# Feed-forward of a decoder trunk: units 4 and 5 with one level of Winograd's scheme in place of two, and three bundles of VectorE work dealt out over the products

## The chip, the cores and the metric

One core of a Trainium2 chip runs the whole program. Its engines work side by side, each through its own list of instructions in the order in which they were written: TensorE (PE, with its weight loads shown as PEld), VectorE (DVE), ScalarE (ACT), GpSimd (POOL) and SyncE (SP). The metric is the device time of one execution in microseconds, lower is better.

## The reference, cut to what matters

```python
for i in range(DEPTH):                                   # 2 layers
    h = rms_norm(x, mix_norm[i])
    x = x + (short_conv_mixer(h, ...), dilated_attention_mixer(h, ...))[i % 2]
    h = rms_norm(x, ffn_norm[i])
    x = x + (silu(h @ w_gate[i]) * (h @ w_up[i])) @ w_down[i]
return rms_norm(x, final_norm)
```

There are 1024 tokens of width 1024, in float32. `w_gate` and `w_up` are 1024 x 2816, `w_down` is 2816 x 1024. The change touches the product of `h` with `w_gate` and `w_up` in the two feed-forwards; the convolution and the attention between them keep their code.

## The kernel before, in words

Every float32 operand is split in a high and a low part (`split`, L128 to L140: ScalarE copies the high part at L138, VectorE subtracts it from the operand at L139, which leaves the low part), and each product of two operands is made of three matmuls: high by high, high by low, low by high (L533, L534, L535).

**Units.** 22 units cover the 2816 columns of the two matrices: unit `u` is 256 columns, of `w_gate` for an even `u` and of `w_up` for the odd `u` after it, multiplied with all tokens. A unit is not computed directly but by Winograd's form of Strassen's scheme: the weights and the tokens are cut in two by two blocks, and seven products of sums of blocks, numbered 1 to 7, replace eight products of blocks. One such product, written (unit, number) here, is 128 columns of weights by 512 rows by 512 tokens: four blocks of rows by three matmuls, so 12 matmuls of 512 columns each. `summed` (L193) makes the sums of weight blocks (L186, `combo`), `part` (L204) splits them (into a tile `w`). The sums of token blocks, the seven operands `self.b[m]`, are made once per feed-forward.

**Two levels.** `whole` (L575) computes a unit with one level, all seven products. The units 0 to 3 of each feed-forward are of this kind. From unit 4 on, two units go together: `shallow` (L597) makes the products 1, 6, 5, 7 and 3 of each, and the products 2 and 4 of both units are made by a second level of the same scheme (`deeper`, L614; its products stand in the order as 11 to 17). A second-level product is 12 matmuls of 256 columns (L625, L627, L628). Its weight operands are sums of quarter blocks (L230), all eight of which are issued when product 5 of the odd unit is prepared (`early`, L243), and its token operands are made out of `self.b[2]` and `self.b[4]` by `deepen` (L637): sums at L641, which the source calls `deep`, then splits into tiles `t` and back into a part of `b`, one step of this generator after each product.

**Evacuation.** After a product ScalarE saves a bank of PSUM where a later product goes on adding to it (`save`, L537 and L539, tile `part`), VectorE adds banks to saved tiles (`add`, L542 and L543; L611 in `shallow`), ScalarE applies Silu to the gate's results (L1137) and VectorE multiplies gate and up (L1140). When all four blocks of a pair of units are there, `store` (L688) makes four sums of them (L704) for the next matrix product and sends them to DRAM from GpSimd's queue (L715). `run(self.store(...))` at L1141 issues these four sums in one go.

**What sets the order.** Nothing is scheduled by a machine. `unit_order` (L252) lists the products; `products` (L561) walks the list. Before product `n` is issued, `take` (L167) has the weights of the products up to `n + 2` prepared (in `deeper` up to three more), so a product's `w` stands on ScalarE's and VectorE's lists two to three products ahead of its matmuls, behind whatever else was issued until then. After product `n`, `filled` (L784) lets each generator in `prep` take one step: `deepen(2)` is put there ten products ahead of (3, 4) (L789), `deepen(4)` one ahead of it (L791).

Counted from 0 in each feed-forward, the products that matter here are: 17 is (1, 3), 18 to 20 are (2, 6), (2, 5), (2, 7), then (3, 6), (2, 4), (2, 3), (3, 5), (3, 7), (4, 1), (3, 4), (3, 3), and 29 to 36 are (4, 6), (4, 5), (4, 7), (5, 1), (4, 3), (5, 6), (5, 5), (5, 7). Product 37, (5, 11), is the first of the second level; the last product of the units is (21, 14), number 180.

## Time and profile before

| what | value |
|---|---|
| median of 3 runs | 2198.8 us (2198.76 to 2199.12) |
| profiled execution, its own time | 2194.63 us |
| its span, first to last instruction | 2192.6 us |
| busy: PE, DVE, ACT, POOL | 2133.3, 1759.4, 999.8, 161.9 us |
| mean granted TensorE clock | 0.992 of full speed |
| first feed-forward, first product to first down product | about 352.6 to 778 us |
| second feed-forward, the same | about 1538 to 1959 us |

A row of the timeline gives the start from the span's beginning, the length, engine, line, operation, tiles written and read, shapes, the number of merged instructions, and in brackets how long the engine sat idle before it and which instruction ended that. Matmuls are pipelined: the length shown is longer than the distance from one start to the next, so their price is read from starts. A row of the windows gives a stretch, its length, the busy time of each engine in it with the number of instructions, the granted TensorE clock, and the load on the DMA engines. The waits list says who waited for whom: total, times, longest.

### The profile page before, as it was taken

The page shows a single profiled execution, that of the slowest core. Times are in us where ns is not written, and L with a number is a line of the kernel's source. Part 1 is how long each engine was busy: PE and PEld are TensorE (multiplying, and loading weights), DVE is VectorE, ACT ScalarE, POOL GpSimd, SP SyncE. Part 2 cuts the span into 40 slices and gives each one's busy share as a digit, 9 for nine tenths or more (in the row PEclk, how much of TensorE's full clock was granted, in tenths as well). Part 3 has the DMA queues.
Part 4 walks back from the last instruction along what each step waited for, and adds up shares of the span by engine and source line. Part 5 has one row for each costly group of instructions (what it writes and reads, how often), then busy time and mean ns, then how long its engine had stood idle before and what let it go on. Part 6 is the DMA issues. An engine that isn't in the chain of part 4 may idle for free.

```text
span 2192.6 us, 30554 instructions
## 1 busy us (share of the span) xinstructions
PE 2133.3 (97%) x11138; PEld 1821.9 (83%) x11138; DVE 1759.4 (80%) x3239; ACT 999.8 (46%) x1812; POOL 161.9 (7%) x212
## 2 busy tenths in 40 slices
PE   7899999999999999999999999999999999999998
PEld 6788888778888878878999999887778888888887
DVE  7797848988888798965677777769988888889886
ACT  6433426444443444434455555525544444454435
POOL 0000001010101000010111111110000101000000
PEclk9999999999999999999999999999999999999999
DMA  4122543222323374423333333544223333365432
GB/s 155 54 83 75 204 156 92 97 92 97 120 97 120 93 280 144 132 82 132 91 91 91 91 91 84 170 124 165 71 77 106 108 103 107 100 234 194 159 91 78
DMA packets 133568, 259.50 MB, mean 118 GB/s; under 512 B 47642, under 2 KB 58922, under 8 KB 133418
## 3 DMA queue, kind: packets, MB, share of 16 engines
q1 hardware_dynamic: 75978, 184.80, 26.1%
q0 software_dynamic: 16272, 49.65, 6.4%
q10 hardware_dynamic: 41168, 23.10, 3.5%
q8 instruction: 88, 1.44, 0.3%
q14 instruction: 62, 0.51, 0.1%
HBM read 187.04 MB, written 66.26 MB: 116 GB/s over the span
## 4 chain that ended last, share of the span: by engine, by line
PE 78%; DVE 13%; ACT 4%; DMA 3%; issue 2%; ACTq 0%; SPq 0%; DVEq 0%
PE bank L533 15%; PE bank L535 15%; PE bank L534 15%; PE bank L349 5%; PE bank L347 5%; PE bank L348 5%; PE bank L1463 4%; PE bank L625 3%; PE bank L627 3%; PE bank L628 3%; DVE w L139 2%; DVE b L526 1%; DVE combo L186 1%; PE bank L1391 1%; PE bank L1390 1%
## 5 line engine op out<-in xcount | busy, mean ns | idle before, releaser
L533 PE MATMUL bank<-b,w 128*128 128x512 f32 x1784 | 704.6, 395 | 25.7 <-DVE part L543 6.4
L535 PE MATMUL bank<-b,w 128*128 128x512 f32 x1784 | 700.7, 393 | 8.7 <-DVE w L139 8.7
L534 PE MATMUL bank<-b,w 128*128 128x512 f32 x1784 | 701.2, 393 | 0.0
L533 PEld LDWEIGHTS bank<-b,w 128*128 128x128 f32 x1784 | 338.8, 190 | 102.1 <-ACT part L539 7.5
L535 PEld LDWEIGHTS bank<-b,w 128*128 128x128 f32 x1784 | 338.7, 190 | 84.1 <-DVE w L139 12.7
L534 PEld LDWEIGHTS bank<-b,w 128*128 128x128 f32 x1784 | 338.5, 190 | 69.7 <-issue 0.7
L138 ACT ACTIVATE w<-combo 128x512 fp32r<-128x512 f32 (+2 forms) x464 | 234.5, 534 | 281.2 <-DVE combo L186 275.2
L139 DVE TENSOR_TENSOR w<-combo,w 128x512 fp32r<-128x512 f32 (+2 forms) x464 | 260.2, 574 | 57.6 <-ACT w L138 56.0
L539 ACT ACTIVATE part<-bank 128x512 f32<-128x512 f32 x168 | 99.5, 593 | 270.2 <-PE bank L535 265.1
L139 DVE TENSOR_TENSOR w<-raw,w 128x512 fp32r<-128x512 f32 (+2 forms) x316 | 169.1, 559 | 17.2 <-ACT w L138 15.6
L543 DVE TENSOR_TENSOR part<-part,bank 128x256 f32<-128x256 f32 (+1 forms) x348 | 158.5, 485 | 26.5 <-PE bank L535 14.3
L138 ACT ACTIVATE w<-raw 128x512 fp32r<-128x512 f32 (+2 forms) x316 | 150.6, 519 | 46.4 <-PE bank L535 11.2
L754 DVE TENSOR_TENSOR x<-x,bank 128x512 f32<-128x512 f32 x168 | 114.2, 680 | 31.1 <-PE bank L535 31.0
L347 PE MATMUL bank<-w_hi,w 128*128 128x512 f32 (+1 forms) x320 | 119.8, 374 | 2.6 <-ACT w L138 2.6
L349 PE MATMUL bank<-w_hi,w 128*128 128x512 f32 (+1 forms) x320 | 118.1, 369 | 0.7 <-DVE w L139 0.7
L348 PE MATMUL bank<-w_lo,w 128*128 128x512 f32 (+1 forms) x320 | 117.8, 368 | 0.0
L466 DVE TENSOR_TENSOR x<-x,bank 128x512 f32<-128x512 f32 (+1 forms) x104 | 66.0, 641 | 60.5 <-PE bank L349 52.2
L186 DVE TENSOR_TENSOR combo<-raw 128x512 f32<-128x512 f32 (+1 forms) x160 | 102.9, 643 | 3.8 <-DMA raw<-in_conv_w_in 3.8
L347 PE MATMUL bank<-h_hi,w_hi 128*128 128x512 f32 x256 | 104.6, 409 | 0.0
L349 PE MATMUL bank<-h_hi,w_lo 128*128 128x512 f32 x256 | 100.2, 391 | 0.7 <-DVE w_lo L139 0.7
L348 PE MATMUL bank<-h_lo,w_hi 128*128 128x512 f32 x256 | 99.9, 390 | 0.0
L1137 ACT ACTIVATE part<-part 128x512 f32<-128x512 f32 x66 | 39.7, 628 | 109.7 <-DVE part L543 109.7
(249 smaller groups left out, 3835.2 us busy)
## 6 DMA issues: line engine op xcount, KB each, us to landing
hin<-part SPq DMA_DIRECT2D x126, 256.0 KB
raw<-in_ffn_w_gate SPq DMA_DIRECT2D x44, 512.0 KB
raw<-in_ffn_w_up SPq DMA_DIRECT2D x44, 512.0 KB
part<-sum POOLq DMA_DIRECT2D x72, 256.0 KB, 2.7
raw<-in_ffn_w_down SPq DMA_DIRECT2D x48, 384.0 KB
x<-spill SPq DMA_DIRECT2D x24, 512.0 KB
raw<-in_attn_w_qkv SPq DMA_DIRECT2D x24, 512.0 KB
raw<-in_conv_w_in SPq DMA_DIRECT2D x21, 512.0 KB
```

Of the source, the lines that this page charges most:

```text
L138: nc.scalar.activation(hi, src, AF.Copy)
L139: eng.tensor_tensor(out=lo, in0=src, in1=hi, op=ALU.subtract)
L186: eng.tensor_tensor(out=c, in0=a, in1=b, op=op)
L347: nc.tensor.matmul(b, whi[:, a], ahi[:, s], start=first, stop=False)
L348: nc.tensor.matmul(b, whi[:, a], alo[:, s], start=False, stop=False)
L349: nc.tensor.matmul(b, wlo[:, a], ahi[:, s], start=False, stop=last)
L533: nc.tensor.matmul(b, hi[:, a], bhi, start=start and k == 0, stop=False, skip_group_check=True)
L534: nc.tensor.matmul(b, hi[:, a], blo, start=False, stop=False, skip_group_check=True)
L535: nc.tensor.matmul(b, lo[:, a], bhi, start=False, stop=k == n - 1, skip_group_check=True)
L539: nc.scalar.activation(t, b, AF.Copy)
L543: nc.vector.tensor_tensor(out=t, in0=t, in1=b, op=ALU.add)
L754: nc.vector.tensor_tensor(out=X[n][:, half(h)], in0=X[n][:, half(h)], in1=b, op=ALU.add)
```

## The change

Five edits, all in the feed-forward's products:

1. `SIMPLE = 6` takes the place of the constants 3 and 4 that bounded the one-level units. Units 4 and 5 become one-level units: products 2 and 4 of each are made whole, and the 14 entries of their second level fall away. Second-level pairs are now (6, 7) to (20, 21), eight per feed-forward where there were nine. The list of products has 178 entries where it had 181.
2. `deepen(2)` is put in after (2, 7) and `deepen(4)` after (4, 5), that is after products 20 and 30 where it was 17 and 26. The last step of each, which overwrites a part of `b`, waits until the last one-level product that reads that operand, (5, 2) or (5, 4), has been issued.
3. The sums of quarter blocks (now L231) are no longer made in one go: one fourth when product 5 of the odd unit is prepared, and one fourth after each of the second level's weights 1, 2 and 5.
4. `store` yields once before its first sum. What is left of it goes into a queue `self.sums`, of which `filled` takes one step after each product, so the four sums (now L712) and their transfers come over the five products that follow.
5. The distances at which weights are loaded from DRAM for units 4 and 5 follow the one-level rule.

```diff
+SIMPLE = 6
...
+        steps = zip(*[sums_of(j, m) for j, m in enumerate(DEEP)])
+
         def part(i):
             load_raw(upto(i))
             w = page("w", F32R)
-            return [split(source(m, i), (w[:, j * HALF:j * HALF + 256], w[:, j * HALF + 256:j * HALF + HALF]),
-                          nc.vector)
-                    for j, m in enumerate(DEEP)]
+            w = [split(source(m, i), (w[:, j * HALF:j * HALF + 256], w[:, j * HALF + 256:j * HALF + HALF]),
+                       nc.vector)
+                 for j, m in enumerate(DEEP)]
+            if i in DEEP_ORDER[:3]:
+                next(steps)
+            return w
 
         def early(op):
             w = op()
-            run(*[sums_of(j, m) for j, m in enumerate(DEEP)])
+            next(steps)
             return w
...
-            for u in range(4, nu, 2):
+            for u in range(4, SIMPLE):
+                order += [(u, 6), (u, 5), (u, 7), (u + 1, 1), (u, 2), (u, 4), (u, 3)]
+            for u in range(SIMPLE, nu, 2):
                 order += [(u, 6), (u, 5), (u, 7), (u + 1, 1), (u, 3), (u + 1, 6), (u + 1, 5), (u + 1, 7)]
...
-            if u < 4 or key == CONV:
+            if u < SIMPLE or key == CONV:
                 a = ((2, 5), (3, 7), (4, 7), (4, 9))[u] if u < 4 else (2 * u + 3, 2 * u + 3)
...
-                ahead = {m: 2 * u + a for m, a in {1: 0 if u > 4 else 3, 6: 1, 5: 2, 7: 3, 3: 3}.items()}
+                ahead = {m: 2 * u + a for m, a in {1: 0, 6: 1, 5: 2, 7: 3, 3: 3}.items()}
...
-            if key != CONV and u > 4 and u % 2:
+            if key != CONV and u > SIMPLE and u % 2:
                 add_deep(units[u], key, u, [[base + r - 2 * (1 - v) for r in rows] for v in range(2)],
...
-                elif self.key != CONV and u > 3:
+                elif self.key != CONV and u >= SIMPLE:
                     self.shallow(u, m, d)
...
-            while self.now <= self.order.index((3, m)):
+            while self.now <= self.order.index((SIMPLE - 1, m)):
                 yield
...
+            yield
             make(7, b22, b12, ALU.subtract)
             yield
...
                     self.now = n + 1
-                    i = self.order.index((3, 4))
-                    if n == i - 10:
+                    if self.order[n] == (2, 7):
                         prep.append(self.deepen(2))
-                    if n == i - 1:
+                    if self.order[n] == (4, 5):
                         prep.append(self.deepen(4))
                     for p in prep:
                         next(p, None)
+                    if self.sums and not next(self.sums[0], "done") is None:
+                        self.sums.pop(0)
...
             self.products(filled, hooks)
+            while self.sums:
+                run(self.sums.pop(0))
...
-            run(self.store(u // 2, c, g))
+            s = self.store(u // 2, c, g)
+            if next(s, "done") is None:
+                self.sums.append(s)
```

Three places show what this does to the lists of instructions. The first is VectorE's list around the weights of product (2, 7). Before, from the last multiplication of gate and up of units 0 and 1 (L1140) to the low part of those weights, the first L139 here; the L139 behind it is (3, 6):

```order
L1140 TENSOR_TENSOR part<-part 128x512
L704 TENSOR_TENSOR sum<-part 128x512 x2
L704 TENSOR_TENSOR sum<-sum,part 128x512
L704 TENSOR_TENSOR sum<-gate,sum 128x512
L641 TENSOR_TENSOR deep<-b 128x256 x4
L186 TENSOR_TENSOR combo<-raw 128x512
L186 TENSOR_TENSOR combo<-combo,raw 128x512
L139 TENSOR_TENSOR w<-combo,w 128x512
L641 TENSOR_TENSOR deep<-deep 128x512
L641 TENSOR_TENSOR deep<-b 128x256 x2
L139 TENSOR_TENSOR w<-combo,w 128x512
```

The same stretch now; the L140 rows are the weights of (2, 7), (3, 6), (2, 4) and (2, 3):

```order
L1152 TENSOR_TENSOR part<-part 128x512
L712 TENSOR_TENSOR sum<-part 128x512
L187 TENSOR_TENSOR combo<-raw 128x512
L187 TENSOR_TENSOR combo<-combo,raw 128x512
L140 TENSOR_TENSOR w<-combo,w 128x512
L712 TENSOR_TENSOR sum<-part 128x512
L140 TENSOR_TENSOR w<-combo,w 128x512
L712 TENSOR_TENSOR sum<-sum,part 128x512
L187 TENSOR_TENSOR combo<-raw,combo 128x512
L140 TENSOR_TENSOR w<-raw,w 128x512
L551 TENSOR_TENSOR part<-part,bank 128x512
L649 TENSOR_TENSOR deep<-b 128x256 x4
```

Between the multiplication and the weights of (2, 7) stood four sums and four `deep` instructions; one sum is left there, the others follow one to a product, and the `deep` instructions have moved behind the weights of (2, 4).

The second place is ScalarE's list around the save of (5, 6), on which (5, 7) waits. Before (the second L539 here is that save; L1137 is the Silu of a block of unit 4; `t` and `b` are written by `deepen(4)`):

```order
L539 ACTIVATE part<-bank 128x512
L138 ACTIVATE t<-deep 128x512
L138 ACTIVATE w<-combo 128x512
L1137 ACTIVATE part<-part 128x512
L138 ACTIVATE t<-deep 128x512
L138 ACTIVATE b<-deep 128x256 x2
L138 ACTIVATE w<-combo 128x512
L539 ACTIVATE part<-bank 128x512
```

Now (L1149 is Silu, L547 the save of (5, 6)):

```order
L1149 ACTIVATE gate<-bank 128x512
L139 ACTIVATE w<-combo 128x512
L1149 ACTIVATE part<-part 128x512
L139 ACTIVATE t<-deep 128x512
L139 ACTIVATE w<-combo 128x512
L547 ACTIVATE part<-bank 128x512
```

The write into `b` is gone from ahead of the save, and the Silu ahead of it no longer follows an addition that stands on VectorE behind the eight sums of quarter blocks, which unit 5 no longer has.

The third place is VectorE's list where the new order is fullest, behind product (4, 7). Now, from the addition for block (1, 1) of unit 4 on; the L140 rows are the weights of (4, 4) and (4, 3):

```order
L551 TENSOR_TENSOR part<-part,bank 128x512
L649 TENSOR_TENSOR deep<-deep 128x512
L649 TENSOR_TENSOR deep<-b 128x256 x2
L712 TENSOR_TENSOR sum<-gate,sum 128x512
L187 TENSOR_TENSOR combo<-raw,combo 128x512
L140 TENSOR_TENSOR w<-raw,w 128x512
L649 TENSOR_TENSOR deep<-deep 128x512 x2
L187 TENSOR_TENSOR combo<-raw 128x512
L187 TENSOR_TENSOR combo<-combo,raw 128x512
L140 TENSOR_TENSOR w<-combo,w 128x512
```

Before, the stretch with the most in one piece was this one, from the addition for block (0, 1) of unit 3 to the weights of (4, 7):

```order
L543 TENSOR_TENSOR part<-part,bank 128x512
L1140 TENSOR_TENSOR part<-part 128x512
L704 TENSOR_TENSOR sum<-part 128x512 x2
L704 TENSOR_TENSOR sum<-sum,part 128x512
L704 TENSOR_TENSOR sum<-gate,sum 128x512
L641 TENSOR_TENSOR deep<-deep 128x512 x2
L139 TENSOR_TENSOR w<-combo,w 128x512
```

In the new order `deepen(4)` and the sums of units 2 and 3 meet under units 4 and 5, with one sum and one step of `deepen` to a product.

More of the change, by code (lines that the diff above doesn't have):

```diff
@@ L512, in __init__ @@
             self.plain = {f: dram.tile([128, S], F32, name=f"plain_{key}_{f}") for f in range(2 * pairs, tiles)}
-            self.st, self.quads, self.hid, self.deep = {}, {}, {}, {}
+            self.st, self.quads, self.hid, self.deep, self.sums = {}, {}, {}, {}, []
             self.banks = set()
```

## The prediction

> **What bounds the kernel now.** I read the page first, then the list of waits of TensorE, then the timelines of the engines around each long wait inside the two feed-forwards.

> ```profile
> PE 2133.3 (97%) x11138; PEld 1821.9 (83%) x11138; DVE 1759.4 (80%) x3239; ACT 999.8 (46%) x1812; POOL 161.9 (7%) x212
> ...
> PE 78%; DVE 13%; ACT 4%; DMA 3%; issue 2%; ACTq 0%; SPq 0%; DVEq 0%
> ```

> TensorE is the bound, and nearly all that can be won without taking matmuls away is the time in which it waits. The waits of TensorE name the releasers:

> ```profile
> PE bank L535 <- DVE w L139: 8.7, 8, 1.9
> PE bank L533 <- ACT part L539: 5.2, 3, 2.3
> PE bank L625 <- DVE part L543: 4.0, 2, 2.0
> ```

> The first row is the low part of a weight that comes too late, the second a save that has not yet freed a bank for further adding. TensorE's timeline shows where they lie in the first feed-forward. The first of them stands in (2, 7), which starts at 410.06:

> ```profile
> 410.06 0.39 PE L533 MATMUL bank<-b,w 128*128 128x512 f32 x1
> 410.29 0.39 PE L534 MATMUL bank<-b,w 128*128 128x512 f32 x1
> 412.60 0.50 PE L535 MATMUL bank<-b,w 128*128 128x512 f32 x1 [1.92 <-DVE w L139]
> ...
> 442.42 0.39 PE L534 MATMUL bank<-b,w 128*128 128x512 f32 x1
> 443.75 0.50 PE L535 MATMUL bank<-b,w 128*128 128x512 f32 x1 [0.94 <-DVE w L139]
> ...
> 456.94 0.39 PE L535 MATMUL bank<-b,w 128*128 128x512 f32 x1
> 459.58 0.74 PE L533 MATMUL bank<-b,w 128*128 128x512 f32 x1 [2.26 <-ACT part L539]
> 460.12 0.63 PE L534 MATMUL bank<-b,w 128*128 128x512 f32 x1
> ...
> 463.11 0.39 PE L535 MATMUL bank<-b,w 128*128 128x512 f32 x1
> ```

> The three waits stand in (2, 7), (4, 7) and (5, 7). After the third the starts are 0.43 us apart instead of 0.23, and the windows say why: the granted clock is about half there.

> ```profile
> 410.06:464.03 53.97, 48.85 (x205) 39.13 (x204) 45.94 (x88) 22.53 (x45) 3.29 (x7) 0.97 0.19 70
> 1590.90:1644.88 53.98, 48.88 (x206) 39.16 (x205) 45.92 (x88) 22.52 (x45) 3.27 (x7) 0.97 0.20 70
> 459.58:463.11 3.53, 3.52 (x9) 2.77 (x10) 2.39 (x7) 1.79 (x6) 0.00 (x0) 0.52 0.02 5
> 470.00:775.00 305.00, 304.28 (x1668) 265.66 (x1666) 252.80 (x538) 133.66 (x285) 29.15 (x54) 1.00 0.33 113
> ```

> The columns behind the length are busy PE, PEld, DVE, ACT and POOL, then the clock. In the first two stretches, products 20 to 36 of each feed-forward, DVE is busy 45.9 of 54 us, 85%; over the long stretch behind it 83%, and there TensorE waits next to nothing. So it is not the load that makes the three waits but how it is bunched. VectorE's timeline ahead of the first wait:

> ```profile
> 405.93 0.69 DVE L1140 TENSOR_TENSOR part<-part 128x512 f32<-128x512 f32 x1
> 406.65 1.29 DVE L704 TENSOR_TENSOR sum<-part 128x512 f32<-128x512 f32 x2
> 407.86 0.68 DVE L704 TENSOR_TENSOR sum<-sum,part 128x512 f32<-128x512 f32 x1
> 408.58 0.69 DVE L704 TENSOR_TENSOR sum<-gate,sum 128x512 f32<-128x512 f32 x1
> 409.19 1.42 DVE L641 TENSOR_TENSOR deep<-b 128x256 f32<-128x256 f32 x4
> 410.53 0.68 DVE L186 TENSOR_TENSOR combo<-raw 128x512 f32<-128x512 f32 x1
> 411.25 0.69 DVE L186 TENSOR_TENSOR combo<-combo,raw 128x512 f32<-128x512 f32 x1
> 411.86 0.68 DVE L139 TENSOR_TENSOR w<-combo,w 128x512 fp32r<-128x512 f32 x1
> ```

> The engine is never idle here, and the row that TensorE waits for ends at 412.54, behind four sums and four `deep` instructions. The prices are read from starts: 0.60 us an instruction of 512, 0.72 where it reads what the one before wrote, (410.53 - 409.19) / 4 = 0.335 for one of 256.

> **What each wait costs.** One matmul of 512 takes 0.227 us from start to start: 410.29 - 410.06 is 0.23, and twelve of them make 2.72, as these two starts five products apart show.

> ```profile
> 482.33 0.39 PE L533 MATMUL bank<-b,w 128*128 128x512 f32 x1
> 495.93 0.39 PE L533 MATMUL bank<-b,w 128*128 128x512 f32 x1
> ```

> (495.93 - 482.33) / 5 = 2.72. The first wait costs 412.60 - 410.29 - 0.23 = 2.08, the second 443.75 - 442.42 - 0.23 = 1.10, the third 459.58 - 456.94 - 0.23 = 2.41 and the slow starts behind it 463.11 - 459.58 - 8 x 0.227 = 1.71. That is 7.3. The stretch as a whole gives the same and the small rest: it holds 17 products, 17 x 2.72 = 46.24, so 53.97 - 46.24 = 7.73 us are lost in the first feed-forward and 53.98 - 46.24 = 7.74 in the second: 15.5 us.

> **The change, part by part.** *Matmuls.* The second level of units 4 and 5 goes: seven products of twelve 256-column matmuls; four whole products come. The row for the seven, with two 512-column products among them:

> ```profile
> 464.03:479.58 15.55, 15.55 (x110) 14.57 (x108) 13.37 (x30) 6.15 (x15) 0.54 (x1) 1.00 0.36 115
> ```

> The seven cost 15.55 - 2 x 2.72 = 10.11 us, the four whole ones 4 x 2.72 = 10.88. So each feed-forward pays 0.77 us more on the engine that is the bound, 1.5 us in all; there is no cover for it. [...]

> *The first wait.* Ahead of the weights of (2, 7) there is now one sum instead of four, and no `deep` instruction. From the same start, 405.93: the multiplication 0.72, one sum 0.60, two `combo` 1.32, the split 0.68, so the low part is there at about 409.3, and TensorE wants it at 410.29 + 0.23 = 410.5. The wait of 2.08 goes. The three sums follow at one to a product, 0.60 against 2.72.

> *The second wait.* The addition ahead of it reads the bank of (3, 3). From the end of (3, 3) VectorE has an addition, a multiplication, one sum and the split, 0.72 + 0.72 + 0.60 + 0.68 = 2.7 us, and two products, 5.44 us, and two matmuls to do it in. The wait of 1.10 goes, with some 3 us to spare.

> *The third wait.* The save of (5, 6) stood on ScalarE behind this chain:

> ```profile
> 453.38 0.75 DVE L230 TENSOR_TENSOR combo<-raw 128x256 f32<-128x256 f32 x2
> ...
> 456.06 0.68 DVE L543 TENSOR_TENSOR part<-part,bank 128x512 f32<-128x512 f32 x1
> ```

> ```profile
> 456.77 0.63 ACT L1137 ACTIVATE part<-part 128x512 f32<-128x512 f32 x1 [4.72 <-DVE part L543]
> 457.31 0.61 ACT L138 ACTIVATE t<-deep 128x512 fp32r<-128x512 f32 x1
> 457.83 0.70 ACT L138 ACTIVATE b<-deep 128x256 fp32r<-128x256 f32 x2
> 458.44 0.61 ACT L138 ACTIVATE w<-combo 128x512 fp32r<-128x512 f32 x1
> 458.96 0.57 ACT L539 ACTIVATE part<-bank 128x512 f32<-128x512 f32 x1
> ```

> Eight sums of quarter blocks (453.38 to 456.06) delay an addition, the Silu waits for it 4.72 us, and the save comes last. With unit 5 whole the eight sums are not there, and the write into `b` (0.61) comes after (5, 2). The new chain: the addition cannot start before (4, 3) ends; from there addition 0.7, Silu 0.5, a `t` 0.5, a `w` 0.5, save 0.6, about 3 us against 5.44 until (5, 7) starts. The wait of 2.41 goes, and with it the half clock, 1.71. [...]

> *New tight places.* The fullest stretch is the third one shown with the change. Counted from the end of (4, 7): the save takes 0.57 and the hand-over an estimated 0.2, so 0.8; then addition 0.60, three `deep` 0.72 + 0.67, sum 0.60, `combo` 0.60, split 0.60: the low part of (4, 4) is there at 4.6, wanted at 5.9. Two `deep`, two `combo` and a split add 3.1: the low part of (4, 3) at 7.7, wanted at 8.6. Only 0.9 us of cover, but cover. Everywhere else in the new stretch I count at most 3.9 us of VectorE work to a product with lighter ones on both sides.

> *Dealt-out quarter sums and queued sums in the eight pairs that stay.* TensorE waits for nothing between 470 and 775, so nothing is won there. The same instructions are only moved: no sum stands later than the weight that reads it, since a fourth of them is made ahead of each use. What could be lost is in the rivals.

> *The tail.* The last product, (21, 14), waits for an addition, and a half clock follows:

> ```profile
> 776.28 0.36 PE L625 MATMUL bank<-t,w 128*128 128x256 f32 x1 [2.00 <-DVE part L543]
> ```

> ```profile
> 777.12:780.53 3.41, 3.41 (x13) 2.93 (x13) 3.38 (x7) 0.00 (x0) 0.00 (x0) 0.50 1.05 408
> ```

> From the weights of (21, 13) on VectorE's list is unchanged, so this wait of 2 us and its half clock stay, in both feed-forwards.

> **Sum.** 15.5 - 1.5 = 14.0 us less. Against the profiled execution 2194.63 that is 2180.6. The median of the runs stands 4.2 us above the profiled time; I keep that distance: 2198.8 - 14.0 = **2184.8 us**.

> **Rivals.** *A (forecast, 0.80):* all three waits go in both feed-forwards. Its own range is 2181 to 2188: small rests of up to 3 us on one side; on the other two half-clock stretches of 1.7 behind the tail's waits, whose gap of 2.0 us may not set them off every time; the gap of 1.92 in (2, 7) sets off none.

> *B (0.08): a save or a low part is still late under units 4 and 5,* since `deepen(4)`, the sums of units 2 and 3 and one-level work meet there with 0.9 us of cover. If one wait like the third comes back, 2 x 2.41 us are lost again, 2189.6, and with its half clock 2 x 4.12, 2193.

> *C (0.04): the half clock stays.* If the half speed is no consequence of the gap, only the waits go and 2 x 1.71 = 3.4 us come back: 2188. Nothing in the trace speaks for it; against it speaks that the slow starts follow at once, here and at the tail. [...]

> *D (0.04): slower, because sums that leave later hold their buffers longer.* The transfers of the sums now start about four products later, and quarter sums and saves write into the half-size buffers that these free. The page gives the transfer 2.7 us:

> ```profile
> part<-sum POOLq DMA_DIRECT2D x72, 256.0 KB, 2.7
> ```

> A quarter sum that waits for a landing holds up VectorE and with it the weights behind it, in each of the 16 pairs. Above 14.0 / 16 = 0.87 us a pair the kernel is slower than before; a full 2.7 gives 2184.8 + 16 x 2.7 = 2228. Against it: by the lists the next writer of such a buffer stands 17 VectorE instructions or more behind the transfer (14 before, and no wait is seen), some 8 us.

> *E (0.04): no gain, the time returns at the tail.* If the last product waited for a transfer from DRAM that keeps its own pace, what is saved earlier is waited for there: 2198.8 + 1.5 = 2200 at most. Against it: the releaser named there is VectorE, not a DMA.

> **How the numbers follow.** No measurement of this kernel can tell less than about 0.2% (4.4 us) from no change. Faster by more than that, under 2194.4, are A, B and C: 0.92. E lies within 0.2%: 0.04. D is slower: 0.04. The range that holds eight in ten takes A's whole own range, C, the lighter form of B at 2189.6, and 1 us below for the distance between profile and median: 2180 to 2190.

> **What would show it.** In the changed profile: no row of TensorE with an idle bracket between the start of (2, 7) and the last product of the units; 23 products, 62.6 us, from the start of (2, 7) to the start of (6, 6); granted clock 1.00 from the first feed-forward's start to its tail; 72 matmuls fewer, 11066, as long as no records are missing; in the waits, TensorE's total for a late low part down from 8.7 by 2 x (1.92 + 0.94) = 5.7 us and that for a late save from 5.2 by 2 x 2.26 = 4.5. The forecast is wrong if a wait on L551, L547 or L231 rows stands in every pair (D), or if the wait at the last product grows by what was saved (E).

## The result, and the profile after

| | before | after |
|---|---|---|
| median of the runs | 2198.78 us (4 runs) | 2182.83 us (4 runs) |
| lowest to highest | 2197.14 to 2199.12 | 2180.55 to 2183.94 |
| after / before, 95% interval | | 0.9932 (0.992 to 0.9944) |
| profiled execution: time, span | 2194.63, 2192.6 | 2183.27, 2181.5 |

Forecast were 2184.8 us, 2180 to 2190, faster by over 0.2%. The change saves 15.9 us by the medians and 11.4 by the two profiled executions.

The page of after, its line of busy engines and its chain of work:

```profile
PE 2131.4 (98%) x11066; PEld 1820.2 (83%) x11066; DVE 1744.0 (80%) x3179; ACT 998.4 (46%) x1792; POOL 161.7 (7%) x212
...
PE 84%; DVE 7%; ACT 3%; DMA 2%; issue 2%; ACTq 0%; SPq 0%; DVEq 0%
```

72 matmuls are gone: in each feed-forward seven second-level products of twelve leave the list and four whole products of twelve come in. (The 14 second-level entries named with the change are those of both feed-forwards together; each list loses seven.) VectorE's share of the chain went from 13% to 7%, and TensorE's own from 78% to 84%. The waits of TensorE that answer to the three groups quoted of before (line numbers are eight higher in after):

```profile
PE bank L633 <- DVE part L551: 4.0, 2, 2.0
...
PE bank L543 <- DVE w L140: 3.2, 4, 1.4
...
PE bank L541 <- ACT part L547: 0.7, 1, 0.7
```

A late low part fell from 8.7 to 3.2 us, a late save from 5.2 to 0.7, and the tail's 4.0 did not move. The windows over the 23 products from (2, 7) to the start of (6, 6), in the first and the second feed-forward:

```profile
409.53:472.09 62.56, 62.56 (x277) 51.80 (x276) 52.36 (x93) 27.10 (x50) 6.47 (x12) 1.00 0.29 100
1585.65:1648.21 62.56, 62.56 (x277) 51.80 (x277) 52.32 (x93) 27.07 (x50) 6.47 (x12) 1.00 0.28 100
```

TensorE is busy all of the time and the clock is 1.00. VectorE is busy 84% there, against 85% in before's stretch: its work is spread, not less.

For the comparison of all runs the *unit stage* of a feed-forward is measured from one fixed wait, in (0, 4), to the end of the last product but one. In before it begins at the first of these rows, in after at the second; its end is read from the last product, less the wait in front of it.

```profile
388.38 0.50 PE L535 MATMUL bank<-b,w 128*128 128x512 f32 x1 [0.56 <-DVE w L139]
```

```profile
387.87 0.50 PE L543 MATMUL bank<-b,w 128*128 128x512 f32 x1 [0.56 <-DVE w L140]
```

| kernel | unit stage, first / second feed-forward, us | median of runs, us |
|---|---|---|
| before | 385.73 / 385.75 | 2198.8 |
| before, second profile | 385.84 / 385.76 | |
| two levels, quarter sums dealt out | 382.53 / 382.54 | 2192.2 |
| two levels, sums queued | 383.58 / 382.18 | 2191.4 |
| two levels, both | 380.57 / 380.58 | 2186.1 |
| one-level units alone | 379.64 / 379.65 | 2183.4 |
| after, four sums at once | 379.64 / 379.64 | 2184.0 |
| after | 378.74 / 378.77 | 2182.8 |
| after, second profile | 378.76 / 378.77 | 2183.0 |
| after, quarter sums at once | 378.74 / 378.75 | 2182.1 |

After saves 6.99 + 6.98 = 13.97 us in this stage, against a forecast sum of 14.0. The second pair of profiles gives 7.08 + 6.99.

### The profile page after: what moved, and what is told of

It reads as the page before. It is cut to its first block, busy times and chain, and to the rows that moved or that the text cites. A ratio compares the mean times of both kernels' runs of the same rounds, so it can differ in the third digit from the quotient of the medians.

```text
span 2181.5 us, 30382 instructions
## 1 busy us (share of the span) xinstructions
PE 2131.4 (98%) x11066; PEld 1820.2 (83%) x11066; DVE 1744.0 (80%) x3179; ACT 998.4 (46%) x1792; POOL 161.7 (7%) x212
## 3 DMA queue, kind: packets, MB, share of 16 engines
q8 instruction: 88, 1.44, 0.3%
## 4 chain that ended last, share of the span: by engine, by line
PE 84%; DVE 7%; ACT 3%; DMA 2%; issue 2%; ACTq 0%; SPq 0%; DVEq 0%
PE bank L541 18%; PE bank L542 17%; PE bank L543 17%; PE bank L357 5%; PE bank L355 5%; PE bank L356 5%; PE bank L1477 4%; PE bank L636 2%; PE bank L633 2%; PE bank L635 2%; PE bank L1405 1%; PE bank L1404 1%; DVE b L534 1%; DVE w L140 1%; PE bank L1345 1%
## 5 line engine op out<-in xcount | busy, mean ns | idle before, releaser
L541 PE MATMUL bank<-b,w 128*128 128x512 f32 x1816 | 715.6, 394 | 21.9 <-DVE part L551 6.4
L543 PE MATMUL bank<-b,w 128*128 128x512 f32 x1816 | 712.5, 392 | 3.2 <-DVE w L140 3.2
L542 PE MATMUL bank<-b,w 128*128 128x512 f32 x1816 | 712.5, 392 | 0.0
L541 PEld LDWEIGHTS bank<-b,w 128*128 128x128 f32 x1816 | 344.6, 190 | 98.3 <-ACT b L533 6.0
L543 PEld LDWEIGHTS bank<-b,w 128*128 128x128 f32 x1816 | 344.0, 189 | 77.5 <-DVE w L140 5.6
L542 PEld LDWEIGHTS bank<-b,w 128*128 128x128 f32 x1816 | 344.3, 190 | 70.8 <-DVE b L844 0.7
L139 ACT ACTIVATE w<-combo 128x512 fp32r<-128x512 f32 (+2 forms) x448 | 229.3, 539 | 252.7 <-DVE combo L187 237.4
L140 DVE TENSOR_TENSOR w<-combo,w 128x512 fp32r<-128x512 f32 (+2 forms) x448 | 254.8, 582 | 45.9 <-ACT w L139 45.6
L547 ACT ACTIVATE part<-bank 128x512 f32<-128x512 f32 x168 | 100.0, 596 | 315.6 <-PE bank L543 309.1
L140 DVE TENSOR_TENSOR w<-raw,w 128x512 fp32r<-128x512 f32 (+2 forms) x312 | 172.1, 570 | 32.8 <-ACT w L139 32.7
L551 DVE TENSOR_TENSOR part<-part,bank 128x256 f32<-128x256 f32 (+1 forms) x328 | 154.4, 500 | 42.8 <-ACT part L547 26.3
L139 ACT ACTIVATE w<-raw 128x512 fp32r<-128x512 f32 (+2 forms) x312 | 151.3, 527 | 45.3 <-PE bank L543 12.5
L1500 ACT ACTIVATE z<-bank 64x512 f32<-64x512 f32 x32 | 19.0, 593 | 141.4 <-PE bank L1477 141.4
## 6 DMA issues: line engine op xcount, KB each, us to landing
hin<-part SPq DMA_DIRECT2D x126, 256.0 KB
part<-sum POOLq DMA_DIRECT2D x72, 256.0 KB, 2.3
```

The lines of the kernel that those rows point to most:

```text
L139: nc.scalar.activation(hi, src, AF.Copy)
L140: eng.tensor_tensor(out=lo, in0=src, in1=hi, op=ALU.subtract)
L541: nc.tensor.matmul(b, hi[:, a], bhi, start=start and k == 0, stop=False, skip_group_check=True)
L542: nc.tensor.matmul(b, hi[:, a], blo, start=False, stop=False, skip_group_check=True)
L543: nc.tensor.matmul(b, lo[:, a], bhi, start=False, stop=k == n - 1, skip_group_check=True)
L547: nc.scalar.activation(t, b, AF.Copy)
```

## The experiments

The theory: three waits with three causes. The four sums and the four `deep` instructions stand ahead of (2, 7)'s low part, the sums ahead of (4, 7)'s, and eight quarter sums hold up the save that (5, 7) waits for. The rival is one backlog of VectorE, which any relief clears.

### Two levels with both halves of the dealing

```
-SIMPLE = 6
+SIMPLE = 4
-    {1: 0, 6: 1, 5: 2, 7: 3, 3: 3}
+    {1: 0 if u > 4 else 3, 6: 1, 5: 2, 7: 3, 3: 3}
...
-    if self.order[n] == (2, 7):
+    i = self.order.index((3, 4))
+    if n == i - 10:
         prep.append(self.deepen(2))
-    if self.order[n] == (4, 5):
+    if n == i - 1:
         prep.append(self.deepen(4))
```

> The changed kernel, but with two levels in units 4 and 5 again and deepen put in where it was before; the sums for DRAM stay in the queue and the quarter sums stay dealt out. Theory (the waits came from bundles on VectorE's list): ahead of the weights of (2, 7) stand one sum and four deep instructions, 0.6 + 1.34 us, so they are there at 410.6 and wanted at 410.5: a wait of 0.1; the wait of 1.10 in (4, 7) stays away; ahead of the addition that holds up the save of (5, 6) stand two quarter sums instead of eight, 2.0 us less, so of the wait of 2.41 in (5, 7) some 0.4 is left, too short for a half clock. The matmuls are 1.5 us cheaper than in the changed kernel, the rests cost 1.0: 2182.3 us, not to be told from the changed kernel. Rival (the room that the one-level units make is what removes the waits): the wait in (5, 7) comes back with 2 us or more and half clocks, 2 x 4.1 - 1.5 = 6.7 us more than the changed kernel, 2189 to 2190.

Measured: 2186.07 us (2185.81 to 2188.23), ratio to before 0.9952 (0.9937 to 0.9967). The unit stage saves 5.2 us a feed-forward. Without the one-level units the dealing already clears most of the three waits. TensorE's rows with an idle time over 0.15 us between the start of (2, 7) and that of the last product in the first feed-forward:

```profile
418.84 0.50 PE L543 MATMUL bank<-b,w 128*128 128x512 f32 x1 [0.20 <-DVE w L140]
...
446.12 0.50 PE L541 MATMUL bank<-b,w 128*128 128x512 f32 x1 [0.24 <-DVE c L619]
...
455.11 0.50 PE L541 MATMUL bank<-b,w 128*128 128x512 f32 x1 [0.47 <-ACT part L547]
```

They stand in (2, 3), (4, 3) and (5, 7); (2, 7) and (4, 7) have none. By starts of matmuls less the usual 0.227 they lose 0.36, 0.40 and 0.63 us, and no half clock follows. Against after this kernel lacks 1.8 us a stage, though it has the cheaper matmuls. Its 2186 lies between what the theory (2182.3) and the rival (2189 to 2190) expected, by the time a little nearer to the rival. The trace is on the theory's side: no wait of 2 us and no half clock at (5, 7). But the theory had the remains too small and missed two places.

### The two halves of the dealing apart

The same kernel, once with the four sums made at once again, once with the quarter sums made at once again:

```
-            s = self.store(u // 2, c, g)
-            if next(s, "done") is None:
-                self.sums.append(s)
+            run(self.store(u // 2, c, g))
```

```
-            if i in DEEP_ORDER[:3]:
-                next(steps)
             return w
...
             w = op()
-            next(steps)
+            run(steps)
```

> Units 4 and 5 have two levels and the deepening starts where it did before; of the change only the quarter sums dealt out over several products are kept, and the four sums for DRAM are made in one go again. Theory (the third wait came from the eight quarter sums in one go, the first two from the four sums in one go): the waits of 2.08 in (2, 7) and 1.10 in (4, 7) stay, that of 2.41 in (5, 7) shrinks to under 0.7 and no half clock follows it, so 2 x (1.7 + 1.7) = 6.8 us of before's 2198 are saved, about 2191. Rival (the three waits are one backlog, and either half of the dealing clears it): all three shrink to under 0.7, 2186, as with both halves. Rival (the third wait comes from the four sums too): nothing is saved, 2198.

> Units 4 and 5 have two levels and the deepening starts where it did before; of the change only the queue of sums for DRAM is kept, and the eight quarter sums are made in one go again. Theory: the waits in (2, 7) and (4, 7) shrink to 0.4 each at most, that in (5, 7) stays at about 2.4 with its half clock of 1.7, so 2 x 2.4 = 4.8 us of before's 2198 are saved, about 2193. Rival (one backlog, either half clears it): 2186, no wait over 0.7. Rival (only the two together help): 2198, the three waits as before.

Measured: 2192.18 us, ratio 0.9972 (0.9958 to 0.9986), with the quarter sums dealt out; 2191.44 us, 0.9972 (0.9961 to 0.9984), with the sums queued. TensorE's timeline of the first of the two:

```profile
411.79 0.50 PE L543 MATMUL bank<-b,w 128*128 128x512 f32 x1 [1.91 <-DVE w L140]
...
442.95 0.51 PE L543 MATMUL bank<-b,w 128*128 128x512 f32 x1 [0.94 <-DVE w L140]
...
456.79 0.50 PE L541 MATMUL bank<-b,w 128*128 128x512 f32 x1 [0.25 <-ACT part L547]
```

The first two waits stand there as in before (1.92 and 0.94), the third is down from 2.26 to 0.25. With the sums queued it is the other way round:

```profile
419.92 0.50 PE L541 MATMUL bank<-b,w 128*128 128x512 f32 x1 [0.20 <-DVE w L140]
...
458.20 0.79 PE L539 MATMUL bank<-b,w 128*128 128x512 f32 x1 [2.48 <-ACT part L545]
```

(2, 7) and (4, 7) have no row with a wait (the first row here is in (2, 3)), and the third wait has its full length. Each half clears its own waits and leaves the others to a tenth of a microsecond or two: the rival falls. These two runs show the causes of the waits. In the second feed-forward of the queued kernel no half clock follows the third wait, which is why its two stages differ by 1.4 us.

### One-level units without the dealing, and after with one half undone

The edits are the two shown above, made to after: both, the first alone, the second alone.

> The changed kernel with only its one-level units 4 and 5 and the later deepen; sums for DRAM and quarter sums both in one go as before. Theory: the same as with the sums in one go alone, a wait of 0.7 in (2, 7), none in (4, 7) and (5, 7): 2184.2 us. Rival (the parts need each other): a wait in (5, 7) or (7, 7) of 2 us or more, 4 to 8 us more, 2188 to 2192.

> The changed kernel, but the four sums of a pair of units are made in one go again. Theory: ahead of the weights of (2, 7) stand four sums, 2.5 us, instead of one, 0.6, and no deep instruction: there at 411.2, wanted at 410.5, so a wait of about 0.7 in each feed-forward; at (4, 7) the list takes 4.7 of the 5.9 us that there are, so no wait; in the eight pairs that follow no wait either. 1.4 us more than the changed kernel, 2184.2. Rival (the queue is what removed the first two waits): waits of 2.1 and 1.1 as before, 2 x 3.2 = 6.4 us more, 2189.

> The changed kernel, but all eight sums of quarter blocks are made in one go again. Theory: the first pair with a second level is now (6, 7), where no step of deepen is left to meet them, and the pairs from 470 to 775 had them in one go before without a wait: no wait of TensorE between (2, 7) and the last product, 2182.8 us give or take 1. Rival (the eight sums caused the wait of 2.41 by themselves): a wait of up to 2 us in (7, 7) of each feed-forward, 4 to 8 us more, 2187 to 2191.

Measured: 2183.38 us, ratio 0.9938 (0.9923 to 0.9953); 2184.03 us, 0.994 (0.9924 to 0.9957); 2182.05 us, 0.9929 (0.9914 to 0.9944). TensorE's timeline of the first, in (2, 7):

```profile
411.83 0.50 PE L541 MATMUL bank<-b,w 128*128 128x512 f32 x1 [0.60 <-DVE w L140]
```

The one-level units with the later deepening clear the three waits nearly alone: the four `deep` instructions that no longer stand ahead of (2, 7) are 4 x 0.335 = 1.34 us, and the wait there is 1.92 - 0.60 = 1.32 shorter. What the queue still adds is the rest, 0.9 us a stage; dealing out the quarter sums adds nothing that can be measured once units 4 and 5 are whole. The one-level units and the later deepening were not tried apart, so which of the two clears the second and the third wait is not shown. The parts of the change overlap: 10.3 us for the dealing, 12.2 for the units, 14.0 for all, in the two stages together.

### Before and after, each profiled a second time

> The kernel before, unchanged, profiled a second time. Theory: the waits in (2, 7), (4, 7) and (5, 7) belong to the program and stand there again within 0.1 us (2.08, 1.10, 2.41), in both feed-forwards; what changes from one execution to the next is the stage between 1457 and 1540 and which of the waits a half clock follows, since the half clock comes in windows of 3.41 us on a grid of its own. A window in which TensorE idles 2.1 us or more is followed by one at half clock, a wait of the same length that the grid cuts in two is not. Rival: the three waits themselves vary by more than 0.5 us between executions, and the saving measured is partly chance. Time 2194 to 2199.

> The kernel after, unchanged, profiled a second time on the same chip as the two others. Theory: 2182 to 2184, no wait of TensorE between the start of (2, 7) and the last product in either feed-forward, and at the tail 2.17 and then 1.6 with one half clock window behind the first, or 2.17 and then 3.2 with the half clock behind the second, as the windows fall. Rival (the waits at the units come back in some executions): a wait of over 1 us there.

Measured: before 2196.93 us in its one run; after 2182.96 us (2180.08 to 2186.28), ratio 0.9932 (0.9916 to 0.9948). TensorE's timeline and windows of before's second profile in the first feed-forward, from the first and from the third wait on:

```profile
413.48 0.50 PE L535 MATMUL bank<-b,w 128*128 128x512 f32 x1 [1.92 <-DVE w L139]
...
462.12 0.50 PE L533 MATMUL bank<-b,w 128*128 128x512 f32 x1 [2.29 <-ACT part L539]
```

```profile
413.48:417.01 3.53, 3.53 (x9) 2.79 (x10) 3.50 (x7) 0.53 (x2) 0.00 (x0) 0.57 0.00 0
462.12:465.65 3.53, 3.53 (x18) 3.01 (x19) 2.39 (x7) 2.24 (x7) 0.00 (x0) 1.00 0.02 5
```

The waits are the same to 0.04 us in both feed-forwards, but in this one the half clock follows the first wait and not the third; in the second feed-forward it follows the third, as in before's first profile. The rival of chance waits falls; what belongs to the execution is which wait the half clock follows. The grid that the theory named is counted out at the end.

After's two profiles have no wait at the units. At the tail its first profile shows both patterns, one in each feed-forward (timeline of TensorE, then windows from the first wait on and, last, the half clock behind the wait of 3.01):

```profile
768.77 0.36 PE L633 MATMUL bank<-t,w 128*128 128x256 f32 x1 [2.01 <-DVE part L551]
...
781.65 0.47 PE L541 MATMUL bank<-b,w 128*128 128x512 f32 x1 [1.48 <-ACT b L533]
...
1944.93 0.36 PE L633 MATMUL bank<-t,w 128*128 128x256 f32 x1 [2.01 <-DVE part L551]
...
1957.80 0.77 PE L541 MATMUL bank<-b,w 128*128 128x512 f32 x1 [3.01 <-ACT b L533]
```

```profile
768.77:772.70 3.93, 3.93 (x16) 3.58 (x17) 3.90 (x9) 0.14 (x1) 0.00 (x0) 0.57 1.02 403
1944.93:1948.46 3.53, 3.53 (x21) 3.19 (x22) 3.50 (x8) 0.31 (x1) 0.00 (x0) 1.00 1.02 406
1957.12:1963.95 6.83, 6.15 (x15) 4.83 (x16) 6.83 (x13) 4.55 (x10) 0.00 (x0) 0.50 0.84 337
```

The same wait of 2.01 halves the clock once and leaves it alone once. Where it does not, TensorE reaches the next wait 1.5 us earlier and waits 1.5 longer there: VectorE, busy 24.93 of 25 us in both tails (765 to 790 and 1941 to 1966), sets the pace. But this longer wait is followed by 6.83 us of half clock, and that is not taken up: 300 matmuls behind the start of (21, 14) TensorE is 71.55 us on in the first feed-forward and 72.98 in the second. In after's second profile both tails go the second way.

### The tail: the low parts of the down projection earlier

VectorE in after, busy time in the whole products of unit 21 and in the tail behind them:

```profile
740.00:757.00 17.00, 17.00 (x83) 14.35 (x83) 9.91 (x23) 7.67 (x17) 0.00 (x0) 1.00 0.32 93
765.00:790.00 25.00, 21.51 (x99) 17.67 (x97) 24.93 (x49) 12.21 (x25) 1.62 (x3) 0.93 0.91 342
```

It idles 7 of 17 us, and then not at all for 25, in which TensorE idles 3.5. The operands of the down projection are made by the generator `feed`, out of tiles `hin`: the low parts come three to a step, 0.60 us each on VectorE. Three placements of the feed's steps in `run` were tried, each made to after, then a mixture:

```
-    if self.order[n][0] == last and n >= self.at(last, DEEPER + 6) - self.base:
+    if self.order[n][0] == last and n >= self.at(last, DEEPER + 1) - self.base:          # three products earlier
+    if self.order[n] in ((last - 1, 3), (last, 6), (last, 5), (last, 7), (last, DEEPER + 4)):   # at the whole products
+    if self.order[n] in ((last, 1), (last - 1, 3), (last, 6), (last, 5), (last, DEEPER + 4)):   # one product earlier still
+    if self.order[n] in ((last, 1), (last - 1, 3), (last, 6), (last, DEEPER + 7), (last, DEEPER + 4)):   # two triples ahead
         next(feed, None)
```

> The kernel after, with the operands of the down projection prepared three products earlier: the feed starts behind (21, 11) instead of (21, 16). VectorE idles 7 of the 17 us from 740 to 757 and never from 765 to 790, where TensorE waits 2.17 and 1.64 us in both feed-forwards. Theory (the tail waits for a backlog of VectorE made of the low parts, three at a time): nine low parts, 9 x 0.60 = 5.4 us, move into the idle time, both waits shrink to under 0.5 and no half clock follows: 2 x (1.7 + 1.2 + 1.7) = 9 us less than after's 2183, about 2174. Rival (the earlier pages and transfers take the place of the last weights, or the low parts wait for their transfers): the waits only move ahead of (21, 17), 2183 or slower.

Measured: 2188.77 us, ratio to before 0.9966 (0.9953 to 0.9979): 6 us slower than after. My theory's placement was wrong. VectorE's windows and timeline:

```profile
740.00:757.00 17.00, 17.00 (x83) 14.35 (x82) 9.90 (x23) 7.67 (x17) 0.00 (x0) 1.00 0.25 70
```

```profile
760.05 0.75 DVE L551 TENSOR_TENSOR part<-part,bank 128x256 f32<-128x256 f32 x2
760.71 1.89 DVE L534 TENSOR_TENSOR b<-hin,b 128x512 fp32r<-128x512 f32 x3
```

Not one low part moved into the idle time, since on VectorE's list they stand behind (21, 12)'s additions, the L551 row here at 760.05. They came at 760.71, ahead of additions that free banks, and TensorE's waits went to (21, 17) and (21, 14):

```profile
766.88 0.55 PE L633 MATMUL bank<-t,w 128*128 128x256 f32 x1 [2.88 <-DVE part L551]
...
773.62 0.55 PE L633 MATMUL bank<-t,w 128*128 128x256 f32 x1 [2.31 <-ACT w L139]
```

> The kernel after, with the first steps of the feed behind (20, 3), (21, 6), (21, 5) and (21, 7) and the fifth behind (21, 14). The run before showed why three products earlier did not help: the low parts came onto VectorE's list behind (21, 12), where its idle time is over, three (1.8 us) to a product of 1.44 us a level. Here nine of them stand behind the whole products of unit 21, 2.72 us each, where VectorE idles. Theory (the tail waits for VectorE's backlog): from 765 on 5.4 us less are queued on it, the waits of 2.17 and 1.64 shrink to under 0.5 and no half clock follows, 2 x (1.7 to 2.2 + 1.1 to 1.6 + 1.7) = 9 to 11 us less than after's 2183, 2172 to 2174. Rival (the low parts spill over into the second-level products, whose sums they delay): a wait of 1 to 2 us appears in (21, 12) to (21, 17), 2180 to 2184.

> As the run with the first steps behind (20, 3), (21, 6), (21, 5) and (21, 7), but one whole product earlier still: behind (21, 1), (20, 3), (21, 6) and (21, 5), the fifth again behind (21, 14). Theory: the same waits go, and nothing spills over into the second-level products, so it is the faster of the two or equal, 2171 to 2174. Rival (the transfers of hin and the buffers held longer delay the saves of (21, 6) to (21, 3) or the weights): a new wait before 757, 2180 or slower.

Measured: 2183.62 us, ratio 0.9935 (0.9922 to 0.9949), no faster than after; 2179.75 us, 0.9917 (0.9903 to 0.9931). In the first of them the rival held, with a longer wait than it named: 4.04 us at (21, 16) replaced the others. One product earlier it is 2.47, and VectorE is busier in the whole products, 11.93 us of 17 (timeline of TensorE in the first run, then timeline and windows of the second):

```profile
763.50 0.55 PE L633 MATMUL bank<-t,w 128*128 128x256 f32 x1 [4.04 <-DVE part L551]
```

```profile
763.69 0.35 PE L633 MATMUL bank<-t,w 128*128 128x256 f32 x1 [2.47 <-DVE part L551]
...
771.17 0.36 PE L633 MATMUL bank<-t,w 128*128 128x256 f32 x1 [0.20 <-DVE part L551]
```

```profile
740.00:757.00 17.00, 17.00 (x79) 14.15 (x79) 11.93 (x22) 10.73 (x23) 0.00 (x0) 1.00 0.51 153
765.00:790.00 25.00, 24.74 (x126) 20.82 (x126) 24.56 (x53) 11.73 (x25) 1.63 (x3) 1.00 0.74 265
```

The second run fits neither its theory (2171 to 2174) nor its rival (a wait before 757). Its first low parts come at 750.33 and the third three only at 756.05, behind which VectorE is busy 7.97 of the 8 us to 765; the idle time ahead of 750 stays unused. So six low parts find room there and nine do not. The mixture keeps six:

> As the run whose first feed steps stand behind (21, 1), (20, 3), (21, 6) and (21, 5), but with the fourth behind (21, 17): only six low parts are made ahead, the three of m = 6 between (21, 17) and (21, 14). In that run TensorE lost 0.28 + 2.63 us ahead of (21, 16), behind three full triples of low parts on VectorE, 0.36 at (21, 14), and nothing of what after loses behind it. Theory (each triple ahead of (21, 16) costs its 1.8 us there once VectorE's idle time is used up): the 2.91 shrinks by 1.8 to about 1.1, the product at 782, for which 1.8 us were to spare, stays without a wait, and no half clock follows: 2 x 1.8 to 2 x 1.8 + 1.7 less than that run's 2179.8, 2174.5 to 2176.2. Rival (the tail has no room left): a wait of about 1.8 us comes back at (21, 14) or behind it, 2179 to 2181.

Measured: 2177.36 us (2176.58 to 2177.75), ratio 0.9907 (0.9891 to 0.9924). TensorE's timeline in the tail:

```profile
761.46 0.36 PE L633 MATMUL bank<-t,w 128*128 128x256 f32 x1 [1.03 <-DVE part L551]
...
768.94 0.36 PE L633 MATMUL bank<-t,w 128*128 128x256 f32 x1 [0.20 <-DVE part L551]
...
780.01 0.47 PE L541 MATMUL bank<-b,w 128*128 128x512 f32 x1 [1.21 <-ACT b L533]
```

The loss ahead of (21, 16), by starts of matmuls, shrank from 2.91 to 1.19 us, as expected, but a part of the rival is true: a wait of 1.21 came back at 780, so the room that I had counted there was not there, and the time is a little over the 2174.5 to 2176.2 expected. No half clock follows any of the tail's waits now. This version beats both kernels, after by 5.5 us; its slowest run (2177.75) is below the fastest of after's eight (2180.08).

## Why the prediction was right

- *Matmuls, +0.77 a feed-forward.* Right. The 23 products take the foretold 62.6 us (62.56), 72 matmuls are gone, and the stage as a whole saves 6.99 where 7.73 - 0.77 = 6.96 was worked out.
- *The first wait.* Right in its working. VectorE's timeline of after, ahead of (2, 7), which starts at 409.53:

```profile
405.42 0.69 DVE L1152 TENSOR_TENSOR part<-part 128x512 f32<-128x512 f32 x1
406.14 0.69 DVE L712 TENSOR_TENSOR sum<-part 128x512 f32<-128x512 f32 x1
406.75 0.69 DVE L187 TENSOR_TENSOR combo<-raw 128x512 f32<-128x512 f32 x1
407.47 0.69 DVE L187 TENSOR_TENSOR combo<-combo,raw 128x512 f32<-128x512 f32 x1
408.08 0.68 DVE L140 TENSOR_TENSOR w<-combo,w 128x512 fp32r<-128x512 f32 x1
```

  From the multiplication to the end of the split are 408.76 - 405.42 = 3.34 us; 409.3 - 405.93 = 3.4 was worked out.
- *The second and third wait.* Right: both are gone, and the two halves of the dealing, tried apart, show that the causes were the ones named. The prediction left out that the dealing alone would nearly do: it is worth 10.3 of the 14.0 us without any one-level unit.
- *The tight place.* Right, with 0.77 us of cover where 0.9 was counted. The last rows of VectorE ahead of (4, 3):

```profile
446.08 0.69 DVE L140 TENSOR_TENSOR w<-raw,w 128x512 fp32r<-128x512 f32 x1
446.69 1.41 DVE L649 TENSOR_TENSOR deep<-deep 128x512 f32<-128x512 f32 x2
...
449.34 0.69 DVE L140 TENSOR_TENSOR w<-combo,w 128x512 fp32r<-128x512 f32 x1
```

  The low part is there at 450.03; (4, 3) starts at 450.33 and wants it two matmuls later, at 450.8. Rival B would have needed this cover to go. The hand-over that was put at 0.2 us took 0.20: (4, 7) ends at 442.17, and its save starts at 442.37.
- *The half clock, 1.71.* Right in size and wrong in its tie to one wait. "The gap of 1.92 in (2, 7) sets off none" held for that execution alone: in before's second profile it sets off one and the gap of 2.29 behind it sets off none. Each of before's four unit stages on record holds one half clock, so the sum stood, but that is luck in part: in the kernel with the sums queued a third wait of 2.48 us has none behind it in the second feed-forward. Rival C, by which the waits have nothing to do with it, falls: a half clock appears behind them and none in after's units.
- *The tail.* The wait of 2.0 stayed to a hundredth, as foretold. That the half clock always follows it did not hold. Where it doesn't, the next wait takes up the 1.5 us, and one half-clock window or two follow that one; two cost 1.4 us more. Rival E falls with the unchanged wait.
- *Buffers held longer, D.* No wait of the named kind between 470 and 768; the stage of the eight pairs keeps its time, and in after's whole list of VectorE's waits no sum of quarter blocks (L231) waits for a transfer.
- *The distance of 4.2 us to the median.* This step failed, though it cost nothing. It was taken as a property of the kernel and is one of the execution: before's second profiled run is 0.9 us below the median of the runs beside it, after's two are 0.4 and 3.3 above theirs. The four profiled executions hold 1421.1, 1423.3, 1424.0 and 1426.7 us outside the two unit stages (before, before, after, after). Two pieces of this are half clocks. Behind the second wait of the tail two windows in a row follow in none, one, one and two of the two tails, at 1.3 to 1.4 us each. And from the first product of the second feed-forward to the fixed wait in (0, 4) before's two profiles take 39.4 us, with 3.41 us of half clock on the way, and after's two 41.0, with 6.83; whether the change brings that or the place of the windows stays open. The two pieces make 3.0 us between the profiled executions of the table, which differ by 11.4 us and not by 14.0. The medians of the table differ by 15.9; over all runs on record, 41 of before and 8 of after, they differ by 14.9. What lies above the 14.0 of the unit stages the traces don't show, and with an interval of 12.3 to 17.6 us on the saving it may be chance. That stays open.

## What to carry to other kernels

A wait that sits behind a burst on a full engine goes when the burst is dealt out in pieces smaller than one product, even if the engine's total load stays at 84%; find the burst by reading backwards from the late instruction on the releaser's own list. Two edits that aim at the same waits don't add up, so sum over waits and not over edits. To move work into another engine's idle time, look where the instruction will stand in that engine's list: three products earlier in the program put it ahead of the additions that TensorE waited for, and cost 6 us.
